# One modulation group of the second layer computed in the first layer's retention stage instead of the expert V stage

## The chip, the cores and the metric

The kernel runs on one core of a Trainium2 chip. The metric is the device time of one execution in microseconds (us). All times below come from the profile page of the kernel before, from its trace, or from its timed runs. Engines are named as the profile names them: PE (TensorE matmul), PEld (its weight loads), DVE (VectorE), ACT (ScalarE), POOL (GpSimd), SP (the queue from which weights are loaded).

## The reference, cut to what matters

The reference is a trunk of two layers on 256 tokens of width 1024. Each layer has a mixer (retention in layer 0, a spatial gating unit in layer 1) and a PEER expert mixer. Six vectors of 1024 numbers per layer (shift, scale and gate, once for the mixer and once for the expert mixer) come from the conditioning vector `c` alone:

```python
c_act = jax.nn.silu(c)
for layer in range(DEPTH):
    mod = c_act @ ada_w[layer] + ada_b[layer]          # (1, 6 * 1024)
    sh1, sc1, g1, sh2, sc2, g2 = jnp.split(mod, 6, axis=-1)
    h = modulate(rmsnorm(x, norm_mix[layer]), sh1, sc1)
    y = retention_mixer(h, ...) if layer % 2 == 0 else sgu_mixer(h, ...)
    x = x + g1[:, None, :] * y
    h = modulate(rmsnorm(x, norm_ffn[layer]), sh2, sc2)
    x = x + g2[:, None, :] * peer_ffn(h, ...)
```

Nothing but `c` stands before a modulation vector, so each of the twelve may be computed at any time before its first use. One of them needs 4 MB of `ada_w`. The vector that the change moves is the scale `sc1` of layer 1, which is first used when layer 1 begins.

## The kernel before, in words

The core streams all weights once from memory in tiles of 128 x 1024 float32 (512 KB). `weight_order` (line 93) lists the tiles, and `weight` (line 181) keeps two tiles ahead of the one in use. `split_load` (line 155) issues the load of a tile on SP (line 161, three `raw` buffers), casts it into `hi` on ACT (line 164) and takes the rest `lo = raw - hi` on DVE (line 165), again with three buffers each. PE multiplies the three products hi*hi, hi*lo, lo*hi.

The stages of a layer follow one another: the norm, the mixer, the norm, and the expert mixer with its query stage, its U stage (with the one-hot gathers in its second part) and its V stage. In the retention stage four heads each take eight tiles of `ret_vg` (two calls of `proj_nat`, line 411, four tiles each) and four tiles of `ret_out` (`project`, line 550; those of a head run in the turn of the next one). In the V stage (line 1138) 60 units of two expert tiles each run in the order of `peer_v_order`: 17 natural ones, and then a mixture whose rows POOL gathers by index (`fetch`, line 1069) up to four units ahead.

The modulation vectors are filler work. The generator `ada` (line 284) makes a vector in nine steps. Eight of them load one tile `adaw` on SP (line 289) and multiply and add it on DVE (line 291 for the first, line 293 for the seven others); each of these DVE instructions also waits for the last matmul that had been written down when the step was asked for (`paced`). The ninth step transposes the sum with eight PE instructions (line 301) and reduces it with two on DVE (line 302) and one addition (line 303). `adaw` has two buffers, so a load waits for the step two before it.

- In the retention stage the filler makes three vectors of layer 0, that is 27 steps. `vg` takes two steps after each `proj_nat`, and `project` one after each of its tiles for the first three heads, which gives 28 places. What is left is taken in line 573.
- In the V stage of layer 0 the generator `adag` (line 1050) makes the last vector of layer 0 and then two of layer 1, again 27 steps, one per unit from the 14th unit on (line 1173). In layer 1 it makes a single vector, nine steps, in the same places.

The program order is not the order on an engine: the framework places instructions by a model of their times when the kernel is built. That order is then fixed, and each engine and each DMA queue works through its own in sequence.

Of the kernel before, what the change touches and what calls it, by code (L numbers as in the profile page):

```python
# [126 lines left out]
def trunk(ctx: ExitStack, tc: tile.TileContext, I, out):  # L127
# [5 lines left out]
    hpool = ctx.enter_context(tc.tile_pool(name="hpool", bufs=2))  # L133
# [7 lines left out]
    def nm(s):  # L141
        uid[0] += 1
        return f"{s}{uid[0]}"

    def ps_tile():
        return work.tile([P, 512], F32, tag="w", name=nm("ps"))

    def acc_tiles():
        return [[acc.tile([P, 512], F32, tag=f"a{b}{n}", name=nm("acc")) for n in range(2)]
                for b in range(NTB)]  # L150
# [72 lines left out]
    def paced(inst, mark=None):  # L223
        return after_mark(inst, mark or marks["gate"])
# [59 lines left out]
    def ada(layer, ks, pool, tag, wtag, bufs=2):  # L284
        for k in ks:
            a = pool.tile([P, 1024], F32, tag=tag, name=nm("ada"))
            for dc in range(DC):
                w = pool.tile([P, 1024], F32, tag=wtag, bufs=bufs, name=nm("adaw"))
                loads.append(nc.sync.dma_start(w, I["ada_w"][layer, k, dc]))
                if dc == 0:  # L290
                    op = nc.vector.tensor_scalar(a, w, c_act[:, 0:1], None, op0=ALU.mult)
                else:
                    op = nc.vector.scalar_tensor_tensor(a, w, c_act[:, dc:dc + 1], a,
                                                        op0=ALU.mult, op1=ALU.add)
                paced(op, marks["pe"])
                yield
            s = mpool.tile([P, DC], F32, tag="adas", name=nm("adas"))
            for n in range(2):
                ps = ps_tile().rearrange("p (m k) -> p m k", m=4)
                for m in range(4):  # L300
                    nc.tensor.transpose(ps[:, m, :], a[:, (n * 4 + m) * P:(n * 4 + m + 1) * P], ident)
                nc.vector.tensor_reduce(s[:, n * 4:n * 4 + 4], ps, axis=AX.X, op=ALU.add)
            nc.vector.tensor_tensor(mod[:, layer, k * 8:k * 8 + 8], s,
                                    ada_b[:, layer, k * 8:k * 8 + 8], op=ALU.add)
            yield
# [64 lines left out]
    def gate_rows(layer, k, scale=1.0):  # L370
        g = hpool.tile([P, D], F32, tag="hl", name=nm("grow"))
        for n in range(2):
            ps = ps_tile()
            for m in range(4):
                dg = mpool.tile([P, P], F32, tag="diag", name=nm("dg"))
                c = k * 8 + n * 4 + m
                nc.vector.tensor_scalar(dg, ones, mod[:, layer, c:c + 1], None, op0=ALU.mult)
                nc.tensor.transpose(ps[:, m * P:(m + 1) * P], dg, ident)
            nc.scalar.mul(g[:, n * 512:(n + 1) * 512], ps, scale)
        return g  # L380

    def residual(b, n, accs, g, xin, xout, pool, tag):
        s = slice(n * 512, (n + 1) * 512)
        tmp = pool.tile([P, 512], F32, tag=tag, bufs=2, name=nm("rtmp"))
        nc.vector.tensor_tensor(tmp, accs[b][n], g[:, s], op=ALU.mult)  # L385
        nc.vector.tensor_tensor(xout[:, b, s], xin[b][:, s], tmp, op=ALU.add)  # L386
# [24 lines left out]
    def proj_nat(name, n, hh, hl):  # L411
        pss = [ps_tile() for _ in range(NTB)]
        for dp in range(4):
            wh, wl = weight(name, n, dp)
            for a in range(2):
                dc = dp * 2 + a
                s = slice(a * 512, (a + 1) * 512)
                for b in range(NTB):
                    tb = slice(b * P, (b + 1) * P)
                    mm3(pss[b], hh[dc][:, tb], hl[dc][:, tb], wh[:, s], wl[:, s],  # L420
                        dc == 0, dc == DC - 1)
        return pss
# [31 lines left out]
    def split_ps(ps, oh, ol):  # L454
        nc.scalar.copy(oh, ps)
        nc.vector.tensor_tensor(ol, ps, f(oh), op=ALU.subtract)

    def retention(xt, pool, filler):
        hh, hl = norm_to_h(xt, 0, 0)
        cos, sin = rope_tables(pool)  # L460

        def fill(n):
            for _ in range(n):
                next(filler, None)
# [22 lines left out]
                dst.append((oh, ol))  # L487
        def vg(hd):
            pss = proj_nat("ret_vg", hd, hh, hl)
            fill(2)  # L490
            vh = pool.tile([P, NTB, DV], F32R, tag="vh", bufs=2, name=nm("vh"))
            vl = pool.tile([P, NTB, DV], F32R, tag="vl", bufs=2, name=nm("vl"))
            for b in range(NTB):
                split_ps(pss[b], vh[:, b, :], vl[:, b, :])
            pss = proj_nat("ret_vg", HEADS + hd, hh, hl)
            fill(2)
            sg = pool.tile([P, NTB, DV], F32, tag="sg", bufs=2, name=nm("sg"))
            for b in range(NTB):
                nc.scalar.activation(sg[:, b, :], pss[b], AF.Silu)
            return vh, vl, sg  # L500
# [47 lines left out]
        accs = acc_tiles()  # L548
# [13 lines left out]
        for hd in range(HEADS):  # L562
            cur = vg(hd)
            nss = scores(hd + 1) if hd + 1 < HEADS else None
            yt = turn(ys) if hd else None
            ys = attend(hd, *ss, *cur)
            ss = nss
            if hd == HEADS - 1:
                grow = gate_rows(0, 2)
            if hd:  # L570
                project(hd - 1, *yt)
# [115 lines left out]
    def peer(layer, xt, hh, hl, xstack):  # L687
# [359 lines left out]

        accs = acc_tiles()
        if layer == 0:
            adag = chain(ada(0, (5,), hpool, "hl", "hh"), ada(1, (1, 0), hpool, "hl", "hh"))  # L1050
        else:
            adag = ada(1, (5,), hpool, "hl", "hh")
        order = peer_v_order()
# [2 lines left out]
        grow = None  # L1056
# [81 lines left out]
        for pos, unit in enumerate(order):  # L1138
# [35 lines left out]
            if pos == len(order) - 6:  # L1174
                drain(adag)
                grow = gate_rows(layer, 5, 1.0 / GSCALE)
# [10 lines left out]
    x = xp.tile([P, NTB, D], F32, tag="x", name="x0")  # L1187
# [7 lines left out]
    for layer in range(2):  # L1195
        with tc.tile_pool(name=f"mixer{layer}", bufs=1) as pool:
            if layer == 0:
                accs, grow = retention(x, pool, ada(0, (2, 4, 3), pool, "ada", "adaw", 2))
            else:
                accs, grow = sgu(x, pool, update)  # L1200
            xs = [x[:, 0], x[:, 1]]
            tag = "zt" if layer else "rt"
            hh, hl = norm_to_h(x, layer, 1,
                               lambda b, n: residual(b, n, accs, grow, xs, x, pool, tag))
        accs, grow, xin = peer(layer, x, hh, hl, xstack)
        xstack = ExitStack()
        xp = xstack.enter_context(tc.tile_pool(name=f"x{layer + 1}", bufs=1))
        x = xp.tile([P, NTB, D], F32, tag="x", name=nm("x"))

        def update(b, n, accs=accs, grow=grow, xin=xin, x=x, xp=xp):  # L1210
            residual(b, n, accs, grow, xin, x, xp, "rtmp")
# [83 lines left out]
```

## Time and profile before

| What | Value |
|---|---|
| Median of three runs | 2140.33 us (2131.61 to 2141.01) |
| The profiled execution | 2121.35 us |
| Its span, first to last instruction | 2119.6 us |
| Mean granted clock of TensorE | 0.976 of full speed |
| Busy share of the span | PE 94%, DVE 79%, ACT 53%, POOL 26% |
| Moved by DMA | 476.62 MB, mean 225 GB/s |

The stages of the span, by the instructions of each: start and first norm up to about 35 us, retention up to about 247 us, query and U stage up to about 719 us, V stage of layer 0 up to 1047 us. Layer 1 follows in the same way, with its V stage from 1780 to 2103 us. A busy share is an average over these stages, so each stage is looked at by itself: how far PE is from being busy without a gap, at which clock, and which wait ends last in front of it. Instructions that the trace merges into one row carry their number as `x8`. A few per cent of the matmul records are missing.

### The profile page before, as it was taken

The page shows a single profiled execution, that of the slowest core. Times are in us where ns is not written, and L with a number is a line of the kernel's source. Part 1 is how long each engine was busy: PE and PEld are TensorE (multiplying, and loading weights), DVE is VectorE, ACT ScalarE, POOL GpSimd, SP SyncE. Part 2 cuts the span into 40 slices and gives each one's busy share as a digit, 9 for nine tenths or more (in the row PEclk, how much of TensorE's full clock was granted, in tenths as well). Part 3 has the DMA queues.
Part 4 walks back from the last instruction along what each step waited for, and adds up shares of the span by engine and source line. Part 5 has one row for each costly group of instructions (what it writes and reads, how often), then busy time and mean ns, then how long its engine had stood idle before and what let it go on. Part 6 is the DMA issues. An engine that isn't in the chain of part 4 may idle for free. (4 is left out here: it accounts for less than half of the span.)

```text
span 2119.6 us, 35127 instructions
## 1 busy us (share of the span) xinstructions
PE 1989.6 (94%) x12988; PEld 1772.8 (84%) x12988; DVE 1678.4 (79%) x3084; ACT 1120.1 (53%) x1894; POOL 540.6 (26%) x493
## 2 busy tenths in 40 slices
PE   4999899999999999999899987999999999999996
PEld 3988799999989877777687776999999898777775
DVE  7877679988989697687677787799889886977665
ACT  2444444445787654454454534444457876545453
POOL 1000001100010336775003600011000103467850
PEclk9999999999999999999999999999999999999998
DMA  7678565556576868898366676555555768798881
GB/s 267 216 247 266 166 186 178 179 185 185 183 244 203 281 215 329 311 338 328 110 208 209 217 273 206 184 179 180 183 188 179 243 195 281 219 330 290 284 279 51
DMA packets 136507, 476.62 MB, mean 225 GB/s; under 512 B 17280, under 2 KB 19344, under 8 KB 135808
## 3 DMA queue, kind: packets, MB, share of 16 engines
q1 hardware_dynamic: 94320, 335.85, 48.1%
q0 software_dynamic: 37392, 128.41, 17.6%
q10 hardware_dynamic: 4608, 9.96, 1.4%
q8 instruction: 105, 1.72, 0.3%
q14 instruction: 82, 0.67, 0.1%
HBM read 438.25 MB, written 35.91 MB: 224 GB/s over the span
## 5 line engine op out<-in xcount | busy, mean ns | idle before, releaser
L164 ACT CAST hi<-raw 128x1024 fp32r<-128x1024 f32 x536 | 561.6, 1049 | 665.2 <-PE ps L210 338.7
L165 DVE TENSOR_TENSOR lo<-raw,hi 128x1024 fp32r<-128x1024 f32 x536 | 674.3, 1260 | 148.3 <-ACT hi L164 129.7
L209 PE MATMUL ps<-hh,hi 128*128 128x256 f32 x2432 | 698.4, 287 | 13.3 <-ACT hi L164 7.8
L211 PE MATMUL ps<-hh,lo 128*128 128x256 f32 x2432 | 690.2, 284 | 2.4 <-DVE lo L165 2.2
L210 PE MATMUL ps<-hl,hi 128*128 128x256 f32 x2432 | 690.9, 284 | 1.3 <-DVE hl L360 1.2
L209 PEld LDWEIGHTS ps<-hh,hi 128*128 128x128 f32 x2432 | 467.6, 192 | 15.2 <-ACT hi L164 8.5
L211 PEld LDWEIGHTS ps<-hh,lo 128*128 128x128 f32 x2432 | 467.2, 192 | 3.4 <-DVE lo L165 3.4
L210 PEld LDWEIGHTS ps<-hl,hi 128*128 128x128 f32 x2432 | 467.8, 192 | 2.1 <-DVE hl L360 2.1
L394 PE MATMUL acc<-lo,wh 128*128 128x512 f32 x672 | 218.9, 407 | 5.4 <-DVE lo L165 4.2
L165 DVE TENSOR_TENSOR lo<-vraw,hi 128x1024 fp32r<-128x1024 f32 x128 | 155.8, 1223 | 78.3 <-ACT hi L164 50.0
L394 PE MATMUL acc<-hi,wl 128*128 128x512 f32 x672 | 213.9, 401 | 0.0
L394 PE MATMUL acc<-hi,wh 128*128 128x512 f32 x672 | 193.9, 406 | 18.9 <-ACT hi L164 9.7
L164 ACT CAST hi<-vraw 128x1024 fp32r<-128x1024 f32 x128 | 134.3, 1050 | 109.6 <-PE acc L394 56.6
L394 PEld LDWEIGHTS acc<-hi,wh 128*128 128x128 f32 x672 | 126.5, 192 | 54.9 <-issue 13.8
L764 POOL TENSOR_TENSOR eq<-eq,tif 128x512 f32<-128x512 f32 x32 | 56.6, 1786 | 450.6 <-DVE eq L759 403.2
L170 POOL DMA_INDIRECT vraw<-in_peer_v,vi x128 | 147.1, 1150 | 89.2 <-issue 31.7
L170 POOL DMA_INDIRECT cell<-w_dram,agi x128 | 153.9, 1202 | 42.0 <-issue 35.4
L394 PEld LDWEIGHTS acc<-lo,wh 128*128 128x128 f32 x672 | 126.1, 192 | 44.5 <-DVE lo L165 14.2
L394 PEld LDWEIGHTS acc<-hi,wl 128*128 128x128 f32 x672 | 128.4, 191 | 30.9
L210 PE MATMUL ps<-lo,hh 128*128 128x512 f32 x320 | 126.3, 395 | 4.0 <-DVE lo L165 4.0
L211 PE MATMUL ps<-hi,hl 128*128 128x512 f32 x320 | 125.8, 393 | 0.0
L914 POOL DMA_DIRECT2D a_dram<-at x52 | 28.4, 546 | 357.0 <-ACT at L807 225.6
(275 smaller groups left out, 2803.7 us busy)
## 6 DMA issues: line engine op xcount, KB each, us to landing
raw<-in_peer_u SPq DMA_DIRECT2D x256, 512.0 KB
raw<-in_peer_v SPq DMA_DIRECT2D x112, 512.0 KB
adaw<-in_ada_w SPq DMA_DIRECT2D x96, 512.0 KB
raw<-in_sgu_in SPq DMA_DIRECT2D x48, 512.0 KB
w_dram<-A POOLq DMA_DIRECT2D x16, 1152.0 KB
raw<-in_ret_vg SPq DMA_DIRECT2D x32, 512.0 KB
raw<-in_peer_q SPq DMA_DIRECT2D x32, 512.0 KB
a_dram<-at POOLq DMA_DIRECT2D x52, 256.0 KB
```

What stands on the lines that cost most here:

```text
L164: after_mark(nc.scalar.copy(hi, raw), after[0], ORDER)
L165: after_mark(nc.vector.tensor_tensor(lo, raw, f(hi), op=ALU.subtract), after[1], ORDER)
L170: nc.gpsimd.indirect_dma_start(out=dst, out_offset=None, in_=table, in_offset=bass.IndirectOffsetOnAxis(ap=index, axis=0))
L209: first = nc.tensor.matmul(ps, ah, bh, start=start, stop=False)
L210: nc.tensor.matmul(ps, ah, bl, start=False, stop=False)
L211: marks["pe"] = nc.tensor.matmul(ps, al, bh, start=False, stop=stop)
L394: marks["pe"] = nc.tensor.matmul(accs[b][n], a[:, tb], bb[:, n * 512:(n + 1) * 512], start=first and a is lh and bb is wh, stop=False)
L764: nc.gpsimd.tensor_tensor(eq, eq, tif[:, :, a, :].unsqueeze(2).to_broadcast([P, NTB, TOPK, TOPK]), op=ALU.mult)
L914: nc.gpsimd.dma_start(a_dram[:, sp * 2:sp * 2 + 2, :], tmp)
```

## The change

The generator of the retention stage gets a fourth vector, group 1 of layer 1, and `vg` takes three steps after each `proj_nat` instead of two: 24 places there and 12 in `project`, 36 for 36 steps. The generator in the V stage of layer 0 loses this group: 18 steps instead of 27, its third vector now standing second. The tile tags in the retention pool are the same, with two `adaw` buffers. The V stage of layer 1 stays as it is.

```diff
         def vg(hd):
             pss = proj_nat("ret_vg", hd, hh, hl)
-            fill(2)
+            fill(3)
...
             pss = proj_nat("ret_vg", HEADS + hd, hh, hl)
-            fill(2)
+            fill(3)
...
         if layer == 0:
-            adag = chain(ada(0, (5,), hpool, "hl", "hh"), ada(1, (1, 0), hpool, "hl", "hh"))
+            adag = chain(ada(0, (5,), hpool, "hl", "hh"), ada(1, (0,), hpool, "hl", "hh"))
...
             if layer == 0:
-                accs, grow = retention(x, pool, ada(0, (2, 4, 3), pool, "ada", "adaw", 2))
+                accs, grow = retention(x, pool, chain(ada(0, (2, 4, 3), pool, "ada", "adaw", 2),
+                                                   ada(1, (1,), pool, "ada", "adaw", 2)))
```

## Rows read from the trace of the kernel before

**Rows 1.** The page: span, and the whole span's busy time by engine.
```profile
span 2119.6 us, 35127 instructions
PE 1989.6 (94%) x12988; PEld 1772.8 (84%) x12988; DVE 1678.4 (79%) x3084; ACT 1120.1 (53%) x1894; POOL 540.6 (26%) x493
```
**Rows 2.** Busy time by window: length, PE, PEld, DVE, ACT, POOL, clock, DMA share, GB/s.
```profile
20.50:30.00 9.50, 6.83 (x40) 6.67 (x40) 9.09 (x18) 0.57 (x1) 0.56 (x1) 1.00 1.03 404
90.00:110.00 20.00, 20.00 (x98) 16.83 (x97) 15.47 (x23) 9.77 (x14) 0.00 (x0) 1.00 0.66 203
150.00:170.00 20.00, 20.00 (x89) 16.49 (x88) 15.44 (x18) 9.35 (x10) 0.00 (x0) 1.00 0.78 273
190.00:210.00 20.00, 20.00 (x96) 16.60 (x95) 15.15 (x18) 8.62 (x10) 0.00 (x0) 1.00 0.83 268
230.00:250.00 20.00, 14.63 (x58) 10.66 (x56) 12.08 (x26) 7.14 (x14) 0.86 (x1) 0.91 0.39 119
550.00:570.00 20.00, 20.00 (x198) 19.66 (x197) 18.79 (x44) 16.90 (x39) 1.10 (x3) 1.00 0.52 162
```
**Rows 3.** The same in the V stage of layer 0; its sum, from 719 us.
```profile
940.00:960.00 20.00, 17.58 (x80) 13.97 (x78) 13.32 (x17) 7.76 (x10) 15.43 (x16) 1.00 0.96 356
960.00:980.00 20.00, 17.82 (x62) 13.24 (x63) 14.75 (x16) 9.94 (x13) 13.74 (x12) 0.83 0.84 304
...
sum 328.20, PE 310.99 PEld 242.05 DVE 243.64 ACT 161.42 POOL 180.21; mean PE 23.92 PEld 18.62 DVE 18.74 ACT 12.42 POOL 13.86
```
**Rows 4.** The same in the V stage of layer 1; its sum, from 1780 us.
```profile
2041.00:2061.00 20.00, 17.09 (x60) 12.87 (x59) 10.29 (x11) 8.99 (x11) 7.97 (x8) 0.83 0.83 304
...
sum 322.90, PE 307.18 PEld 238.21 DVE 221.52 ACT 159.09 POOL 182.46; mean PE 23.63 PEld 18.32 DVE 17.04 ACT 12.24 POOL 14.04
```
**Rows 5.** Timeline: the same two expert tiles' lo on DVE, layer 0, then layer 1.
```profile
950.43 1.21 DVE L165 TENSOR_TENSOR lo<-vraw,hi 128x1024 fp32r<-128x1024 f32 x1
...
966.97 1.23 DVE L165 TENSOR_TENSOR lo<-raw,hi 128x1024 fp32r<-128x1024 f32 x1 [3.23 <-issue]
...
2011.41 1.23 DVE L165 TENSOR_TENSOR lo<-vraw,hi 128x1024 fp32r<-128x1024 f32 x1 [0.65 <-ACT hi L164]
...
2017.28 1.23 DVE L165 TENSOR_TENSOR lo<-raw,hi 128x1024 fp32r<-128x1024 f32 x1 [0.35 <-ACT hi L164]
```
**Rows 6.** Timeline of layer 0 around 945 us: loads on SP, the cast that waited.
```profile
942.34 0.33 SPq L161 DMA_DIRECT2D raw<-in_peer_v  x1
943.53 0.33 SPq L289 DMA_DIRECT2D adaw<-in_ada_w  x1
944.72 0.33 SPq L161 DMA_DIRECT2D raw<-in_peer_v  x1
...
965.89 1.04 ACT L164 CAST hi<-raw 128x1024 fp32r<-128x1024 f32 x1 [4.67 <-remote]
```
**Rows 7.** DMA queues from 940 to 985 us: packets, MB, share of the engines.
```profile
q0 software_dynamic: 2733, 9.30, 57.9%
q1 hardware_dynamic: 1302, 4.73, 28.0%
```
**Rows 8.** Tile adaw: one step on DVE; and a vector's ninth step in the timeline.
```profile
L293 DVE SCALAR_TENSOR_TENSOR ada<-adaw,c_act,ada x84: 1270/1279/1333, 6.9 to 1930.3; 128x1024 f32<-128x1024 f32 x84
946.28 1.03 PE L301 MATMUL ps<-ident,ada 128*128 128x128 f32 x8
947.78 1.28 DVE L302 TENSOR_REDUCE adas<-ps 128x4 f32<-128x512 f32 x2
```
**Rows 9.** Timeline of the retention stage: two matmuls 24 apart; a load, the step on it.
```profile
95.38 0.39 PE L209 MATMUL ps<-hi,hh 128*128 128x512 f32 x1
...
100.82 0.39 PE L209 MATMUL ps<-hi,hh 128*128 128x512 f32 x1
...
216.47 1.65 SPq L289 DMA_DIRECT2D adaw<-in_ada_w  x2
221.44 1.28 DVE L293 SCALAR_TENSOR_TENSOR ada<-adaw,c_act,ada 128x1024 f32<-128x1024 f32 x1 [1.22 <-DMA adaw<-in_ada_w]
```

## The prediction

> **What bounds the kernel now.** I read the page first: PE is busy 94% of the span and no other engine comes near it [rows 1]. So 130 us of the span are without a matmul, and a change that adds no PE work can win only there or where PE runs at the lower of its two clocks. Next I cut the two stages of the change into windows of 20 us. In the retention stage PE is busy for 20.00 of 20 us at the full clock in each of the seven windows from 90 to 230 us, of which three are shown; DVE works 15.2 to 15.5 us and DMA moves 203 to 273 GB/s there [rows 2]. PE alone bounds this stage, and nothing there is late. Only its last window has gaps, 14.63 of 20 us, where the chain of the residual and the norm begins [rows 2]. In the V stage of layer 0 the picture is another. PE loses 2.42 us in the window from 940 and 2.18 us in the one from 960, where its clock is 0.83, and DMA moves 304 to 356 GB/s [rows 3]. The reader is to see a stage whose PE is fed late at times because its transfers are late. The timeline says which: two expert tiles are loaded on SP at 942.34 and 944.72, a modulation tile `adaw` goes between them at 943.53, and the cast of a tile from SP starts only at 965.89 after a wait of 4.67 us [rows 6]. In that stretch the queue of POOL's gathers takes 57.9% of the engines and the SP queue 28.0%, 4.73 MB in 45 us or 105 GB/s [rows 7].
>
> **A comparison inside the trace.** The V stage exists twice. Layer 1 does the same work with 9 filler steps instead of 27: its last multiply of a modulation tile starts at 1930.3 us [rows 8], so from there to its end it has none. From 719 us the stage of layer 0 takes 328.2 us, from 1780 us that of layer 1 takes 322.9 [rows 3, 4]: 18 steps are worth 5.3 us in all. Where in the stage? The same two expert tiles, counted from its start, are split at 950.43 and 966.97 in layer 0, 16.5 us apart, and at 2011.41 and 2017.28 in layer 1, 5.9 us apart [rows 5]. From the first of the two to the end (719 + 328.2 = 1047.2; 1780 + 322.9 = 2102.9) layer 0 takes 96.8 us and layer 1 takes 91.5. The whole difference of 5.3 us lies in the part behind 950 us, and that is where the third vector of layer 0 runs: the ninth step of the second one stands at 946.28 [rows 8]. Layer 1 is not free of stalls there either: 17.09 of 20 us and a clock of 0.83 from 2041 us, with no modulation load at all [rows 4]. So part of the late feeding belongs to the gathers and stays.
>
> **The change part by part: V stage.** The change takes out eight loads of 0.524 MB, eight DVE steps of 1.28 us [rows 8], eight PE transposes of 1.03 us together and two reductions of 1.28 us together [rows 8]. The steps are asked for one per unit in order, so the first 18 stay where they are and the stage is bare of filler from about 947 us on, the state of layer 1 behind 2011 us. The term is therefore the measured difference, 5.3 us, the transposes included. Bounds: at the least the 1.03 us of PE work goes and the stall only moves. At the most both gaps and the slow clock of the windows from 940 to 980 go: 2.42 + 2.18 us, and 0.17 of 20 us that the clock withheld, 3.4 us, and 1.03: 9.0 us. I take 5.3, since it comes from the same work without the same filler.
>
> **Retention stage.** Added are the same eight loads, eight DVE steps, eight transposes and two reductions. On PE, which has no gap, the 1.03 us [rows 8] lie on the path in full. DVE gets 8 x 1.28 + 1.28 = 11.5 us over the 140 us from 90 to 230, which lifts it from 77% to 85%; its cover is the gap between its work and PE's, and a window of the U stage shows PE at 20.00 with DVE at 18.79 [rows 2], so I cost it at nothing. If that cover failed, all 11.5 us would show. DMA gets 4.2 MB more, 30 GB/s over the stage, on 203 to 273; 404 GB/s were moved from 20.5 us on [rows 2]. After a `proj_nat` three tiles follow instead of two. A `proj_nat` is 48 matmuls; 24 of them take 100.82 - 95.38 = 5.44 us [rows 9], so it lasts 10.9 us, and seven tiles (3.67 MB) in that time are 337 GB/s: below what the engines moved, though above what this stage has shown.
>
> Against this speaks the Trainium skill, page "DMA: Bandwidth & Descriptors", section "Bandwidth": it puts the memory's limit for one core at about 358 GB/s, by which those 337 GB/s would leave hardly any room, and loads would come late. The trace disagrees: 404 GB/s in the window from 20.5 us [rows 2]. By the limit of the Trainium skill the seven tiles would still need only 10.2 us of the 10.9, so the sum would be the same and only the slower rival below would gain.
>
> The 36 steps find 36 places, so the drain in front of the last projection has nothing left to do. Layer 1 reads the moved vector only at its start, so no wait of its own follows.
>
> **The sum.** -5.3 + 1.0 = -4.3 us. The profiled execution takes 2121.35 us, of which 1.75 lie outside the span; it would take 2117.1. That execution lies 19 us below the median of the runs, 2140.33 us; I carry the difference over and forecast 2136.0 us.
>
> **The rivals.**
> 1. *The gathers remain the bound.* The stall of layer 0 only moves to another tile, as layer 1 shows one from 2041 us without any filler [rows 4]; 1.0 us leaves and 1.0 us arrives, or the dearer half of DVE's cover in retention (5.7 us) eats the gain. Time 2140, up to 2142. For it: POOL's queue has twice the share of SP's [rows 7]. Against it: the 5.3 us between the twins.
> 2. *The stall vanishes entirely.* -9.0 + 1.0 = -8.0 us: 2132.3. For it: with 105 GB/s for SP's queue each `adaw` tile is worth 5 us of that queue [rows 7], and two fewer ahead of a late tile are more than the whole wait of 4.67 us [rows 6]. Against it: layer 1's own stall. Gains beyond this would need other stalls of the stage to ease too.
> 3. *Slower: the third load in two buffers.* The third load of a place can go only after the first step of that place, which waits for the last matmul of the `proj_nat`. If SP's order puts expert loads behind it, PE has two prepared tiles, 5.4 us [rows 9], against 1.28 for the step, 3.7 to 5.0 for the load (the two loads issued over 1.65 us from 216.47, the wait ended at 221.44 [rows 9]), and 1.04 and 1.23 for cast and rest [rows 5, 6]: 7.3 to 8.5 us. PE would wait 1.9 to 3.1 us at each of eight places, 15 to 25 us, at the lower clock more. With -4.3 that is 2151 to 2161. It decides from the point where a weight load stands behind the third one in SP's order. Against it: a `raw` buffer comes free as soon as its tile is split, one or two tiles ahead of PE, so these loads mostly go first.
>
> **How the numbers follow.** Forecast 0.48, rival 1 0.26, rival 2 0.15, rival 3 0.11. Half a per cent, 10.7 us, is about what a measurement of this kernel can tell from no change; the runs before alone lie 9.4 us apart. Forecast, rival 1 and most of rival 2 fall within it: same 0.72. Faster, below 2129.6, takes a third or more of rival 2 and runs that fall low: 0.16. Slower, above 2151, is rival 3 and little else: 0.12. The range from 2126 to 2150 holds the forecast and the first two rivals with the spread of the runs, and leaves out rival 3 and the far end of rival 2.
>
> **What would show it.** In the profile after, PE should stay at 20.00 in the windows from 90 to 230 us with DVE near 17 and DMA near 300 GB/s at times; the end of retention should come about 1 us later. `adaw` should be absent from SP behind about 937 us, the two tiles of rows 5 should lie nearer 6 than 16 us apart, and the V stage should last about 323 us. PE gaps of 2 us behind each `proj_nat`, with a cast waiting for a `ret_vg` load, would show rival 3; a stall of the same size on a gathered tile would show rival 1. The prediction is wrong if the build places instructions far from these two stages otherwise than before, which no row can exclude.

## The result and the profile after

The changed kernel takes 2152.01 us in the median of five runs (2150.26 to 2154.17); the kernel before, in five runs, takes 2136.64 us (2123.75 to 2141.01). The ratio is 1.0076, with an interval from 1.0049 to 1.0104. It is slower by three quarters of a per cent, 15.4 us in the medians, and it lies outside the range of the prediction, whose upper end was 2150.

The page of the changed kernel, span and busy time by engine, answers to [rows 1]:

```profile
span 2148.9 us, 35112 instructions
PE 1997.5 (93%) x12988; PEld 1780.9 (83%) x12988; DVE 1680.5 (78%) x3084; ACT 1120.2 (52%) x1894; POOL 535.6 (25%) x493
```

PE has the same number of instructions and the span is 29 us longer. PE is busy only 8 us longer, so most of the difference is time in which PE waits. Where it waits, the windows of the retention stage show (columns as in [rows 2]: length, PE, PEld, DVE, ACT, POOL, clock, DMA share, GB/s):

```profile
110.00:130.00 20.00, 18.92 (x86) 15.18 (x84) 15.32 (x26) 8.66 (x14) 1.08 (x2) 1.00 0.81 265
130.00:150.00 20.00, 15.15 (x70) 12.80 (x70) 11.35 (x15) 6.32 (x9) 0.00 (x0) 0.91 0.60 198
150.00:170.00 20.00, 20.00 (x92) 16.19 (x91) 17.40 (x29) 7.77 (x14) 1.09 (x2) 1.00 0.76 254
170.00:190.00 20.00, 17.22 (x86) 14.28 (x85) 14.16 (x18) 8.62 (x10) 0.00 (x0) 1.00 0.82 283
...
210.00:230.00 20.00, 20.00 (x98) 16.65 (x97) 14.72 (x17) 10.16 (x13) 0.00 (x0) 1.00 0.88 309
230.00:250.00 20.00, 16.60 (x77) 12.99 (x77) 17.39 (x32) 8.32 (x13) 1.06 (x2) 0.95 0.70 222
```

Before, each of the windows from 90 to 230 us was full [rows 2]. Now the one from 110 lacks 1.08 us, the one from 130 lacks 4.85 us and has a clock of 0.91, and the one from 170 lacks 2.78 us; the last one, which had gaps before too, shows PE waiting again. DVE is not the bound in any of them: where PE loses most, DVE is busy for 11.35 of 20 us, against 15.99 in the same window before. It is not a shortage of DVE time. DMA moves up to 309 GB/s in windows in which PE is full.

To compare whole kernels I use one stretch, called the head part below: from the first matmul with 512 columns of the first `vg` to the last matmul into `acc` of the retention stage. In the profiled executions it takes 155.7 us before and 172.5 after. The other parts changed little: start of the head part +2.0, from its end to the first matmul of the query stage +3.1, query and U stage +2.8, V stage of layer 0 +3.3, layer 1 up to its V stage -2.5, V stage of layer 1 +3.9. With the +16.8 of the head part that makes the 29.4 us between the two profiled executions (2121.35 and 2150.71).

The waits of PE between 90 and 270 us, changed kernel (engine, tile and line that waited, what it waited for: us in total, times, longest), name the place:

```profile
PE ps L301 <- DVE ada L293: 8.6, 3, 4.8
...
DVE ada L293 <- DMA adaw<-in_ada_w: 7.8, 6, 2.7
```

The first line was not there before: the transposes of a vector's ninth step (line 301) wait for the eighth step on DVE (line 293). Before, these transposes never waited for anything in this stage. The timeline shows it at the worst place, in the changed kernel:

```profile
129.76 0.39 PE L211 MATMUL ps<-hi,hl 128*128 128x512 f32 x1
130.13 0.69 DVE L456 TENSOR_TENSOR vl<-ps,vh 128x512 fp32r<-128x512 f32 x1 [0.32 <-ACT vh L455]
130.73 1.28 DVE L293 SCALAR_TENSOR_TENSOR ada<-adaw,c_act,ada 128x1024 f32<-128x1024 f32 x1
131.93 0.68 DVE L456 TENSOR_TENSOR vl<-ps,vh 128x512 fp32r<-128x512 f32 x1
132.53 1.22 DVE L165 TENSOR_TENSOR lo<-raw,hi 128x1024 fp32r<-128x1024 f32 x1
133.66 1.28 DVE L293 SCALAR_TENSOR_TENSOR ada<-adaw,c_act,ada 128x1024 f32<-128x1024 f32 x1
...
135.00 1.77 PE L301 MATMUL ps<-ident,ada 128*128 128x128 f32 x8 [4.85 <-DVE ada L293]
...
178.07 1.09 PE L301 MATMUL ps<-ident,ada 128*128 128x128 f32 x8 [2.78 <-DVE ada L293]
...
214.38 1.03 PE L301 MATMUL ps<-ident,ada 128*128 128x128 f32 x8
...
246.89 1.06 PE L301 MATMUL ps<-ident,ada 128*128 128x128 f32 x8 [0.96 <-DVE ada L293]
```

The matmul at 129.76 is the last one of a `proj_nat`. Steps 7 and 8 of a vector are asked for right behind it, so `paced` makes both wait for that very matmul: step 7 can't start before 130.15. DVE then works in its own order: a `vl`, step 7, a `vl`, a `lo`, step 8. In PE's order the transposes of step 9 stand directly behind the same matmul, and the next matmuls of the stage stand behind the transposes. So PE sits through a whole trip to DVE and back: 0.69 + 1.28 + 0.68 + 1.22 + 1.28 = 5.15 us of DVE work, of which 4.85 are bare. Then PE works at the lower clock for a while: the eight transposes take 1.77 us and not 1.03.

The four rows also are a dose. With three steps per `proj_nat` and one per tile of `project`, step 9 falls in one place with steps 7 and 8 (4.85 us), step 18 in one place with 17 (2.78), step 27 is the first of its place (no wait), and step 36 has a place of its own directly behind that of 35 (0.96). With two steps per `proj_nat`, as before, steps 9, 18 and 27 fall in `project`, where other work stands between. In the kernel before:

```profile
144.22 0.60 PE L301 MATMUL ps<-ident,ada 128*128 128x128 f32 x4
...
189.48 1.03 PE L301 MATMUL ps<-ident,ada 128*128 128x128 f32 x8
...
228.77 1.04 PE L301 MATMUL ps<-ident,ada 128*128 128x128 f32 x8
```

In the V stage of this profile there is still a stall, in front of another kind of tile than that of [rows 6]. The window from 940 us, the cast and the matmul that waited in it, changed kernel:

```profile
940.00:960.00 20.00, 9.22 (x25) 6.08 (x26) 9.45 (x11) 6.08 (x7) 10.68 (x11) 0.66 0.69 235
```
```profile
952.26 1.04 ACT L164 CAST hi<-vraw 128x1024 fp32r<-128x1024 f32 x1 [9.60 <-remote]
...
953.36 1.22 PE L1104 MATMUL acc<-hi,wh 128*128 128x512 f32 x2 [7.49 <-ACT hi L164]
```

`vraw` is a tile that POOL gathers, not one from SP. PE waits 7.49 us for it, at a clock of 0.66 in that window. The stall stands where modulation tiles are still loaded; the last of them goes out on SP behind it:

```profile
964.65 0.33 SPq L289 DMA_DIRECT2D adaw<-in_ada_w  x1
979.30 69.23 SPq L161 DMA_DIRECT2D raw<-in_peer_v  x9
```

In the part that the change did clear, from 965 to 1050 us, PE is busy without a gap (85.00 of 85 us). So this profile alone speaks neither for the V term of the prediction nor against it.

### The profile page after: what moved, and what is told of

The parts are those of the page before. It is cut to its first block, busy times and chain, and to the rows that moved or that the text cites. A ratio compares the mean times of both kernels' runs of the same rounds, so it can differ in the third digit from the quotient of the medians.

```text
span 2148.9 us, 35112 instructions
## 1 busy us (share of the span) xinstructions
PE 1997.5 (93%) x12988; PEld 1780.9 (83%) x12988; DVE 1680.5 (78%) x3084; ACT 1120.2 (52%) x1894; POOL 535.6 (25%) x493
## 5 line engine op out<-in xcount | busy, mean ns | idle before, releaser
L209 PEld LDWEIGHTS ps<-hh,hi 128*128 128x128 f32 x2432 | 469.8, 193 | 16.5 <-ACT hi L164 8.9
L164 ACT CAST hi<-vraw 128x1024 fp32r<-128x1024 f32 x128 | 134.1, 1050 | 116.9 <-PE acc L394 67.8
L394 PEld LDWEIGHTS acc<-hi,wh 128*128 128x128 f32 x672 | 126.8, 192 | 56.3 <-ACT hi L164 15.4
L293 DVE SCALAR_TENSOR_TENSOR ada<-adaw,c_act,ada 128x1024 f32<-128x1024 f32 x84 | 107.6, 1281 | 19.1 <-DMA adaw<-in_ada_w 16.6
```

The source lines that it names most:

```text
L164: after_mark(nc.scalar.copy(hi, raw), after[0], ORDER)
L209: first = nc.tensor.matmul(ps, ah, bh, start=start, stop=False)
L394: marks["pe"] = nc.tensor.matmul(accs[b][n], a[:, tb], bb[:, n * 512:(n + 1) * 512], start=first and a is lh and bb is wh, stop=False)
```

## The experiments

The theory after this reading: **position**. The loss comes from where the ninth step stands behind a `proj_nat`, not from the amount of work moved. The rivals: **work** (11.5 us of DVE and 4 MB of loads in the retention stage), **buffers** (the third load of a place in two `adaw` buffers), and the **V stage** (the stage with fewer steps is slower or not faster). Ratios are to the kernel before in runs on the same chip. This matters: the kernel before takes 2096 to 2098 us on three chips, and 2135 to 2137 in the runs of the result and those beside ret_only. Of two profiles of it, 2121.35 and 2098.32 us, the whole difference of 23 us lies in the V stages (10.5 and 12.5, below).

The head part in the profile of each kernel, from one window each:

| Kernel | length, us | PE idle, us | clock | PE waits at the ninth steps, us | ratio |
|---|---|---|---|---|---|
| before_again | 154.3 | 1.9 | 1.00 | none | |
| after_again | 173.8 | 14.0 | 0.96 | 8.3 | 1.0110 |
| pace3 | 165.9 | 10.1 | 0.98 | 7.1 | 1.0062 |
| bufs3 | 166.8 | 10.1 | 0.98 | 7.7 | 1.0060 |
| join9 | 170.3 | 12.4 | 0.96 | 10.2 | 1.0079 |
| early8 | 158.3 | 2.9 | 0.99 | none | 1.0020 |
| late3 | 159.3 | 5.4 | 1.00 | 1.5 | 1.0021 |
| late3_bufs3 | 157.9 | 3.9 | 1.00 | 1.5 | 1.0015 |
| nopace | 157.5 | 3.8 | 1.00 | none | 1.0098 |

### The two halves of the change alone

v_only has the new V stage of layer 0 and the old retention stage:

```diff
+    nc.vector.memset(mod[:, 1, 8:16], 0.0)
...
-            adag = chain(ada(0, (5,), hpool, "hl", "hh"), ada(1, (1, 0), hpool, "hl", "hh"))
+            adag = chain(ada(0, (5,), hpool, "hl", "hh"), ada(1, (0,), hpool, "hl", "hh"))
```

> The V stage of the change with the retention stage of before; the vector that the change moves is not computed here at all, its place holds zeros. If the V stage gains what the comparison of its twins promised, the V stage of layer 0 falls from 327.3 us (profile of before) to about 322 and the ratio to before is about 0.9975. If the gathers of POOL bound the stage, as rival 1 had it, the V stage stays within 2 us of 327 and the ratio is 0.999 to 1.001. The retention stage must end at 246 us, as before.

Measured: 1.0019, interval 1.0005 to 1.0033 (2101.18 against 2095.92 us), which is neither case of the expectation. On this chip the V stage with nine steps fewer gains nothing; the kernel is even a little slower. With zeros in the vector's place layer 1 works on other numbers and may gather other rows; its V stage takes 308.6 us, and 311.7 in v_bare below, beside 309.1 to 311.0 in the other profiles from such chips. Its windows from 940 and 960 us are full in this profile, so the stall named in the prediction is absent. That this is no merit of the missing steps, the next section shows.

ret_only has the new retention stage and the old V stage, so the vector is computed twice:

```diff
-            adag = chain(ada(0, (5,), hpool, "hl", "hh"), ada(1, (0,), hpool, "hl", "hh"))
+            adag = chain(ada(0, (5,), hpool, "hl", "hh"), ada(1, (1, 0), hpool, "hl", "hh"))
```

> The retention stage of the change with the V stage of before, so the moved vector is computed twice. This closes the account: the whole change measured 1.011 beside its parts, the V part alone 1.0019 and the V stage without any second-layer filler 0.9992. If the V stage neither gains nor loses, this ratio is 1.010 to 1.012. If the V part by itself really costs 4 us (another arrangement of the gathers), this is 1.008 to 1.0095. If the V stage had gained the 5.3 us of the prediction after all, this would be 1.013 or more.

Measured: 1.0104, interval 1.0065 to 1.0143 (2158.73 against 2135.05 us); its head part takes 172.9 us. The retention half alone loses as much as the whole change does in the next section (1.0110). Whether the old V stage costs something beside it, this run doesn't tell: its interval takes in all three cases of the expectation, and in the runs of the result, where the kernel before is as slow, the whole change cost only 1.0076. This was one of the slower chips, and its V stage has a stall again, at another place than in the two profiles above, with 27 steps in it:

```profile
980.00:1000.00 20.00, 9.69 (x28) 6.64 (x27) 7.55 (x8) 5.24 (x7) 9.81 (x10) 0.66 0.79 272
```

### The two kernels once more, on another chip

Nothing is edited; the point is the spread of the stages between profiles of the same program.

> The kernel before, unchanged, for a second profile of it. If the stages are steady, the head part of retention lasts 155.7 us again (from its first 512-column matmul at 90.4 to 246.0) and the V stages 327 and 322 us. If the V stages vary with how the gathers land, as the profiles so far suggest (309 to 326 us for the same V stage of layer 1), they lie elsewhere while retention is the same within 1 us.

> The changed kernel, unchanged, beside the others on one chip. Expected from the single parts so far (pace alone 1.0062, retention as changed but with later transposes 1.0021): a ratio of 1.006 to 1.009, the head part of retention 171 to 173 us, PE waiting 7 us or more for a DVE step before line 301.

Measured: before 2098.32 us in one execution (the median beside it 2096.51), after 2119.90 us, ratio 1.0110, interval 1.0093 to 1.0127, more than the 1.006 to 1.009 that was expected. The loss repeats, and with it the waits at the ninth steps: 8.3 us in three, the longest 4.8. Head part: 154.3 and 173.8 us. The V stage of layer 0, in which the prediction saw its gain, takes 316.8 us before and 312.7 after. In the first pair of profiles it was 327.3 and 330.6. And the stall of [rows 3] is not there in the kernel before on this chip, with all 27 steps in place (windows of before_again):

```profile
940.00:960.00 20.00, 20.00 (x91) 16.23 (x91) 17.63 (x22) 10.96 (x13) 15.43 (x16) 1.00 1.01 372
960.00:980.00 20.00, 20.00 (x87) 16.09 (x87) 17.44 (x18) 11.71 (x15) 16.04 (x14) 1.00 1.00 350
```

The two windows that lost 4.6 us in [rows 3] lose nothing, at a higher rate of DMA. So the same filler stands beside a stall in one profile and beside none in the other. In the V stage of layer 0 behind 920 us the longest idle time of PE in front of a matmul into `acc` is 3.70, 7.49 and 7.30 us in the three profiles from the slower chips (before, after, ret_only), and under 2 us in all eleven from the faster ones, whatever the number of steps.

### What the steps in the V stage cost

v_bare leaves 18 steps out of the V stage of layer 0 and not nine, with the old retention stage:

```diff
+    nc.vector.memset(mod[:, 1, 0:16], 0.0)
...
-            adag = chain(ada(0, (5,), hpool, "hl", "hh"), ada(1, (1, 0), hpool, "hl", "hh"))
+            adag = ada(0, (5,), hpool, "hl", "hh")
```

> Both second-layer vectors left out of the V stage of layer 0 (their places hold zeros), retention as before: the V stage of layer 0 then has the nine filler steps of layer 1's. If the comparison of the twins was sound, the two V stages now last the same within 1.5 us and the ratio is about 0.995 (two thirds of 27 steps worth 5.3 us, and their 2 us of transposes). If filler is hidden in the V stage and its length is set by how the gathers land, the ratio lies between 0.998 and 1.001, that is at most the 2 us of PE work are gained.

Measured: 0.9992, interval 0.9982 to 1.0002 (2094.52 against 2096.51 us). Eighteen steps are worth 1.7 us, 3.8 at most, where the prediction gave 5.3 to 18 steps of the twins and took the whole of it for the nine that it removed. The V stage of layer 0 in all the profiles from the chips where the kernel before takes about 2097 us: with 27 steps 316.8, 313.7 (pace3) and 313.9 (join9); with 18 steps 320.7 (v_only), 315.6, 313.8, 313.6, 312.7, 312.6 and 312.3; with nine 313.8. The number of steps doesn't order them. On these chips, where the V stage has no long stall, the filler is hidden. Neither v_only nor v_bare was run on a slower chip, so what the steps cost beside a stall is not shown.

### Pace without work

pace3 is the kernel before with three steps per `proj_nat`. No work is moved or added; 27 steps only fall in other places:

```diff
             pss = proj_nat("ret_vg", hd, hh, hl)
-            fill(2)
+            fill(3)
...
             pss = proj_nat("ret_vg", HEADS + hd, hh, hl)
-            fill(2)
+            fill(3)
```

> Everything as before, but three steps after each proj_nat in the retention stage instead of two; no vector is moved. If the pace is the cause (a third load that two buffers let go only after the place's first step, and transposes that stand right behind the steps they need), the retention stage ends at 256 us or later against 246.0 before and 264.9 after the change, with PE waiting for a DVE step before line 301. If the 4 MB more in the stage are the cause, it ends at 246 to 248 us.

Measured: 1.0062, interval 1.0042 to 1.0082, head part 165.9 us. The ninth steps in its timeline:

```profile
133.14 1.97 PE L301 MATMUL ps<-ident,ada 128*128 128x128 f32 x8 [4.83 <-DVE ada L293]
...
176.41 1.09 PE L301 MATMUL ps<-ident,ada 128*128 128x128 f32 x8 [2.30 <-DVE ada L293]
...
212.70 1.03 PE L301 MATMUL ps<-ident,ada 128*128 128x128 f32 x8
```

The same pattern as after the change: 4.83, 2.30, nothing. With no added DVE work and no added load, more than half of the loss is there. That speaks against work and for position; the third load in two buffers is in this kernel too, so the next two runs separate these.

### Position and buffers apart

late3 is the changed kernel with the transposes put off: they are asked for behind the third step of the next vector, as a step of their own. The amount of loads and DVE work, the pace and the two `adaw` buffers stay; the sum tile gets a second buffer, and the first three loads of each next vector are asked for one step earlier:

```diff
+    def ada_late(groups, pool, tag, wtag, bufs, late):
...
+            for dc in range(DC):
+                if dc == late and held is not None:
+                    fold(*held)
+                    held = None
+                    yield
...
-                accs, grow = retention(x, pool, chain(ada(0, (2, 4, 3), pool, "ada", "adaw", 2),
-                                                   ada(1, (1,), pool, "ada", "adaw", 2)))
+                accs, grow = retention(x, pool, ada_late(((0, 2), (0, 4), (0, 3), (1, 1)), pool, "ada", "adaw", 2, 3))
```

`fold` holds the transposes, the reductions and the addition of line 301 to 303.

> The changed kernel, but the eight transposes and the two reductions of a vector are asked for three steps later (line 301), and the sum tile has a second buffer for that; loads and DVE steps stand where the change put them. If PE is held by transposes whose sum is late, those waits (8.6 us in three places in the profile after) and the slow clock behind them go: the retention stage ends near 253 us instead of 264.9. If the third load with two buffers does it by itself, the stage still ends at 261 us or later, with weight tiles and their rests late. If the 4 MB do it, also 261 or later.

Measured: 1.0021, interval 1.0006 to 1.0037, head part 159.3 us. The transposes (now line 313) in its timeline:

```profile
135.72 1.04 PE L313 MATMUL ps<-ident,ada 128*128 128x128 f32 x8
...
171.97 1.03 PE L313 MATMUL ps<-ident,ada 128*128 128x128 f32 x8
...
233.98 1.09 PE L313 MATMUL ps<-ident,ada 128*128 128x128 f32 x8 [1.55 <-DVE ada L331]
```

The transposes still stand behind `proj_nat` calls, but their operands are three steps old, and they wait no longer; 14 of the 19 us by which the head part had grown are gone, with all of the moved work still in place. What is left at 233.98 is the last vector's, which has no next vector to be put off behind.

bufs3 is the changed kernel with three `adaw` buffers and the transposes where they were:

```diff
-                accs, grow = retention(x, pool, chain(ada(0, (2, 4, 3), pool, "ada", "adaw", 2),
-                                                   ada(1, (1,), pool, "ada", "adaw", 2)))
+                accs, grow = retention(x, pool, chain(ada(0, (2, 4, 3), pool, "ada", "adaw", 3),
+                                                   ada(1, (1,), pool, "ada", "adaw", 3)))
```

> The changed kernel with three buffers for the modulation tiles of the retention stage instead of two, so that the third load of a place need not wait for the first step of that place. If the late third load is the root, the DVE waits for modulation tiles (7.8 us after) and most of PE's waits before line 301 go and the retention stage ends at about 250 us. If the position of the transposes in PE's queue is a cause by itself, PE still waits 2 to 3 us before each of three groups of transposes and the stage ends at 256 to 260 us. If the 4 MB do it, it ends at 262 us or later.

Measured: 1.0060, interval 1.0038 to 1.0083, head part 166.8 us. Its waits from 90 to 270 us:

```profile
PE ps L301 <- DVE ada L293: 7.7, 3, 4.8
...
DVE ada L293 <- DMA adaw<-in_ada_w: 0.6, 1, 0.6
```

The third buffer takes DVE's wait for `adaw` from 7.8 us to 0.6, and PE's wait at the transposes hardly changes. So the buffers are a second, smaller cause: some 6 to 7 us of the head part. How they cost it the changed kernel shows in two places, the first before its first hold:

```profile
123.02 1.28 DVE L293 SCALAR_TENSOR_TENSOR ada<-adaw,c_act,ada 128x1024 f32<-128x1024 f32 x1 [2.71 <-DMA adaw<-in_ada_w]
...
126.32 3.49 DVE L165 TENSOR_TENSOR lo<-raw,hi 128x1024 fp32r<-128x1024 f32 x3
...
127.59 0.50 PE L210 MATMUL ps<-lo,hh 128*128 128x512 f32 x1 [1.08 <-DVE lo L165]
```

A step that waits 2.71 us for its tile holds up the `lo` behind it on DVE, and PE waits 1.08 us for that `lo`. The second and larger one is near the end of the head part, where `dg`, the operand of the transposes of `gate_rows`, stands on DVE behind steps that waited 1.89 and 0.68 us for their tiles:

```profile
245.41 0.52 PE L378 MATMUL ps<-ident,dg 128*128 128x128 f32 x2 [2.19 <-DVE dg L377]
```

PE waits there for 2.19 us in this profile, 2.53 in ret_only and 3.04 in after_again, and not at all in bufs3. Of the 3.9 us by which PE's idle time falls from after_again to bufs3, 3.0 are this wait. late3, with two buffers, doesn't have it either, so the two buffers alone don't make it.

late3_bufs3 does both, the put-off transposes and the third buffer:

```diff
-                accs, grow = retention(x, pool, ada_late(((0, 2), (0, 4), (0, 3), (1, 1)), pool, "ada", "adaw", 2, 3))
+                accs, grow = retention(x, pool, ada_late(((0, 2), (0, 4), (0, 3), (1, 1)), pool, "ada", "adaw", 3, 3))
```

> The changed kernel with both: transposes three steps later, and three buffers for the modulation tiles. Later transposes alone gave 159.4 us for the head part of retention and a ratio of 1.0021, three buffers alone 166.8 us and 1.0060. If what is left with later transposes is the late third load, the head part falls to 156 to 157.5 us (1.0 us of transposes is added work) and the ratio to 0.999 to 1.001. If it is the 4 MB or the DVE work, it stays at 159 us or more and 1.002.

Measured: 1.0015, interval 1.0002 to 1.0027, between the two cases of the expectation, head part 157.9 us, 3.6 over before_again. Of these 1.03 are the added transposes and 1.5 the wait that is left at the last vector. That leaves about 1 us for the work itself, 11.5 us of DVE and 4 MB, once it stands well. With the transposes out of the way the third buffer is worth 1.4 us and not 7, and 1.4 us is also what two profiles of the kernel before differ by (155.7 and 154.3): the two causes are not additive.

### The same steps in other places

early8 is the changed kernel with two steps per `proj_nat` again and the other eight behind the tiles of the query and key part, ahead of `vg`:

```diff
                 dst.append((oh, ol))
+                fill(1)
...
-            fill(3)
+            fill(2)
...
-            fill(3)
+            fill(2)
```

> The changed kernel with the fourth vector kept, but its nine steps taken one after each of the eight q and k projections, and two steps after each proj_nat as before. If the place of the steps is the whole loss, the head part of retention lasts 156 to 158 us as before, the q and k part grows by at most 3 us, and the ratio is 0.999 to 1.002. If 4 MB more in the retention stage cost something wherever they stand, the q and k part, whose first tiles are waited for already, grows by 8 us or more and the ratio stays above 1.004.

Measured: 1.0020, interval 1.0005 to 1.0035, head part 158.3 us, and no wait of the transposes from 90 to 270 us. Same work, same two buffers, other places: most of the loss is gone.

join9 goes the other way. It is the kernel before, two steps per place and nothing moved, but the ninth step is asked for together with the eighth:

```diff
                 paced(op, marks["pe"])
-                yield
+                if not (joined and dc == DC - 1):
+                    yield
```

with `joined` true in the retention stage alone.

> The kernel before with one edit: in the retention stage a vector's eighth and ninth step are taken in one place, so that the transposes stand in PE's queue right behind the last matmul of a proj_nat, while the DVE steps they need still wait for that very matmul. Two steps a place, no byte moved, nothing added. If that round trip from PE to DVE and back is the cause, three places hold PE for about 5 us each, the slow clock comes on top, the head part of retention grows from 155 to between 165 and 175 us and the ratio is 1.005 to 1.010. If the pace of three steps or the 4 MB were the cause, nothing of this is here: 154 to 157 us and 0.999 to 1.001.

Measured: 1.0079, interval 1.0058 to 1.0100, head part 170.3 us. The loss is made from the kernel before, without the change's work, without three loads in a place, and all three ninth steps pay:

```profile
140.44 1.10 PE L302 MATMUL ps<-ident,ada 128*128 128x128 f32 x8 [2.80 <-DVE ada L293]
...
185.20 1.97 PE L302 MATMUL ps<-ident,ada 128*128 128x128 f32 x8 [4.71 <-DVE ada L293]
...
228.33 1.09 PE L302 MATMUL ps<-ident,ada 128*128 128x128 f32 x8 [2.72 <-DVE ada L293]
```

Head parts of 154.3 and 170.3 differ by 16.0 us. Idle time of PE rises by 10.5 us, of which 10.2 are these three waits, and its busy time by 5.5 us, at a mean clock of 0.96 and not 1.00.

### Without the pace

nopace is the changed kernel in which the filler of the retention stage no longer waits for the matmul written last:

```diff
-                paced(op, marks["pe"])
+                if pace:
+                    paced(op, marks["pe"])
```

> The changed kernel, but the filler's DVE steps in the retention stage no longer wait for the last matmul written down before them, only for their tile. If the transposes are late because the seventh and eighth step may not begin before the proj_nat ends, the waits of PE in the retention stage before line 302 (the transposes) fall from 8 us to under 3, the head part of retention from 173 to about 160 us, and the ratio from 1.011 to 1.002 to 1.005. If the steps are late because their tiles land late (third load, two buffers), PE waits as before and the head part lasts 168 us or more.

Measured: 1.0098, interval 1.0072 to 1.0123, far from the 1.002 to 1.005 that was expected. The head part is 157.5 us with no wait of the transposes, as position says. But the whole kernel is no faster than the changed one, because the head part starts at 107.4 us and not at about 91. Without the pace the loads of the filler go out early: ten of them on SP between 35 and 65 us, where the changed kernel has two and the next two at 105. They run beside the tiles of the query and key part. Waits from 20 to 108 us in this kernel; in the changed one the first of these lines has 11.5 us in three waits (17.8 in six in the kernel before), and the second isn't there:

```profile
ACT hi L164 <- DMA raw<-in_ret_qk: 25.0, 8, 11.1
...
PE ps L209 <- DVE rb L483: 7.8, 1, 7.8
```

So this run moved steps instead of only freeing them. It bears out that the pace is one leg of the round trip, and shows what the pace is for; as a clean test of position it doesn't count.

## Why the prediction was wrong

**The forecast** was 2136.0 us, 4.3 less than the 2140.33 of the three runs before that were known, and 2152.01 was measured, 15.4 more than the kernel before. The term of the retention stage failed, by far more than its 1.0 us. The V term found no support where it was tested, and is open on the slower chips.

**"its cover is the gap between its work and PE's ... so I cost it at nothing"** is the step that failed first. The cover was read from busy shares: DVE at 77 to 85%, and a U stage with DVE at 18.79 and PE at 20.00. A busy share says that DVE has time in a window. It doesn't say whether PE's next instruction waits for the particular DVE instruction that has been held up. (The 15.2 to 15.5 us of DVE hold for the three windows shown; over all seven they are 14.35 to 16.52. That changes nothing in the sum.) The moved work of DVE was indeed nearly free (late3_bufs3: 1.0015). What cost 8.6 us of PE's wait, and more at the lower clock behind it, were the 8 transposes of each vector standing directly behind the matmul that paced their own operands. The prediction's last clause on the point, "If that cover failed, all 11.5 us would show", had a size near the 15.4 us that were measured, by luck: its reason was not the right one.

**"the 1.03 us [rows 8] lie on the path in full"** was right as far as it went; what was missing is the wait in front of them. The change from `fill(2)` to `fill(3)` was costed as eight more steps. It is also a renumbering: all four vectors get their ninth step in another place. pace3 shows that this alone makes 1.0062. The prediction counted 36 steps and 36 places, and didn't write down which step falls in which place.

**"Layer 1 reads the moved vector only at its start, so no wait of its own follows"** was true of layer 1. The waits that the moved steps have inside the retention stage were weighed in rival 3 alone, for the loads and not for the transposes.

**The V term of -5.3 us** rested on the difference of two like stages in one profile [rows 3, 4]. Between two profiles of the same unchanged program on two chips, each of these stages moves by more than that (327.3 and 316.8; 321.9 and 309.4), and the difference of the twins goes from 5.3 to 7.4. The sign that pointed to the filler moves too: in before_again, with all 27 steps, the two tiles of [rows 5] are split at 950.27 and 958.12, 7.9 us apart and not 16.5. Each beside the kernel before on its own chip, 18 steps are worth 1.7 us and nine steps nothing (v_bare, v_only). But on these chips the stall is absent. On the slower ones the whole change cost 15.4 us and its retention half alone 23.7 (2158.73 against 2135.05), and the intervals of 1.0076 and 1.0104 overlap: a gain of 5 us in the V stage there is neither shown nor excluded. What makes the twins differ is open as well.

**Rival 1**, the gathers remain the bound, is not decided in layer 0: the stall of the profile after is in front of a gathered tile (952.26), as rival 1 had it, but modulation tiles were still being loaded then, up to 964.65. In layer 1 the same profile has waits of 2.58, 3.75 and 2.59 us between 2002 and 2024 us, where the last modulation load went out at 1935.70, so stalls without filler exist. Its time of 2140 gave the retention stage 1.0 us, and 5.7 at most, and so missed the loss.

**Rival 3** gave 2151 to 2161 us and so has the measured time, but only part of its mechanism. The third load in two buffers does cost: 6 to 7 us of the head part (bufs3). Casts do wait longer for `ret_vg` loads, 16.2 us in ten waits against 10.0 in five before, but PE's wait for a cast in the head part is 1.1 us in one place, as before, and not 1.9 to 3.1 us at eight. What costs is that late `adaw` tiles hold up DVE, and through DVE the `lo` of a weight tile and `dg`. The larger part is the ninth step, which no rival had. At 0.11 the chance of this side was too low: the stage to which work was added had PE without a gap, so that each new wait there showed in full.

**The line to watch** was the right one: "PE should stay at 20.00 in the windows from 90 to 230 us" is the line that failed at once and pointed to the place. The loads for the DMA were right too: windows of up to 309 GB/s stand beside a full PE.

Not settled: what the nine steps cost in the V stage of a slower chip; why v_only is 0.2% slower with less to do; where the 2 to 3 us between the head part and the query stage come from, which the changed kernel, pace3 and bufs3 lose and late3 doesn't; and whether any version with the vector in the retention stage beats the kernel before. The best of these, late3_bufs3, is at 1.0015, and with 1.7 us to be had in the V stage for twice the steps there is little to win on the faster chips.

## What to carry to other kernels

Cover is read at the instruction's place in the queue of the engine that sets the end, not from busy shares: an instruction whose operand is released by the instruction directly in front of it costs the whole trip to the other engine and back (here up to 4.85 us, with DVE busy for 11.35 of 20 us). When a pace or a count is changed, write down which step falls in which place before and after, since all steps behind it move too. A difference between like stages of one profile becomes a price only when a second profile of the same program shows it.

## What the runs showed of the hardware

- A wait of 2.78 us leaves the granted clock at 1.00 in its window, and the transposes behind it take 1.09 us. One of 4.85 us is followed by the lower of the two clocks: they take 1.77 us (1.97 in pace3 and join9), the next matmuls 0.77 and 0.63 us instead of 0.39, and the window's mean is 0.91. So the long wait costs more than its length.
- The same program differs by 40 us between chips, 2096 and 2136 us in the medians, while its head part takes 154.3 and 155.7 us. The V stages, with the gathers, differ: 316.8 and 327.3 us in layer 0, 309.4 and 321.9 in layer 1 (profiled executions of 2098.32 and 2121.35). Why, no run here shows.
